# Two products pending behind the rows of the forgetting units, and the first plain gate tile issued in 16 steps behind transposes of the last six attention groups

## The chip, the cores and the metric

The kernel runs on one core of one Trainium2 chip. The metric is the device time of one execution in microseconds. Engines are named as the profile names them: PE (TensorE, the matmuls), PEld (its weight loads), DVE (VectorE), ACT (ScalarE), POOL (GpSimd) and SP (SyncE, which issues the DMAs).

## The reference

One decoder block on x of 1024 positions and 1024 channels, all in float32. Cut to what matters:

```
h = rms_norm(x, g_pre)
proj = h @ w_in
qa, ka, va, fa, za, qb, kb, vb, zb, gates = split(proj)
# forgetting attention (FoX): 8 heads of 64
log_f = log_sigmoid(fa + b_forget); c = cumsum(log_f)
P = softmax(causal(q k^T / 8 + c[t] - c[s]));  ya = (P v) * silu(za)
# differential attention: 4 heads, q1/q2 and k1/k2 of 64 with rope, v of 128
P = softmax(q1 k1^T) - lam * softmax(q2 k2^T);  yb = rms_norm(P v) * (1 - lam_init) * silu(zb)
gate_a, gate_b = split(sigmoid(gates))
merged = gate_a * (ya @ w_branch[0]) + gate_b * (yb @ w_branch[1])
out = x + rms_norm(merged @ w_out, g_post)
```

## The kernel before, in words

**Number format.** A float32 factor is cut into a high part (rounded to the matmul's float32 format, fp32r) and the rest, `hi` and `lo`. A product is three matmuls: hi with hi, hi with lo, lo with hi. So `project` (L242), which multiplies 128 columns of `w_in` with one half of the 1024 positions (a chunk of 512), is 8 x 3 = 24 matmuls of 512 columns. `load_w` (L225) loads such weights and splits them: its two flags say whether ACT or POOL makes `hi`, and whether POOL or DVE makes `lo`.

**Stages.** First x is normalized and transposed into `hT`, and V and the forget gate's logits (`fg`) are projected, to about 100 us. Then come eight attention units of two heads each: units 0 to 3 are differential, units 4 to 7 forgetting units (whose tiles have an f in their names, as the others have a d). The projections of q and k for the next unit, those of z (`z_tasks`, names `pz`, `sz`), and a few other tasks are cut into steps, which the loop at L626 puts between the attention's groups as filler; the list `ZFILL` says which z tiles belong to which unit. The last unit has two of them, z6 and z7. Attention ends at 595.5 us. Then come the gates: for the output tile d = 0 plain products (`gates_plain`, L792: two branches, two chunks, 96 matmuls), for d = 1 to 7 a Winograd scheme with eight combination tiles T that `h_load` (L804) fetches from DRAM. Then the branch products, and the output product to the end.

**A group of attention.** A group is a pair of rows of 128 queries (2g+1 and 2g in the forgetting units), with a weight of 4g+3 in the loop's count. In units 4 to 7 each group g exists for both heads (m = 0, 1), and g falls from 3 to 0. Its name is f, the unit, m, g: `f7_1_2` is unit 7, head 1, group 2. For each row `s_row` (L415) computes the scores in up to two pieces (tiles `S`, a PSUM pool of 3 banks); DVE adds the bias and reduces the minimum out of PSUM into an SBUF tile `P` (a pool of 6); ACT takes the exponential, and POOL scales it. Then `av` (L438) runs, the products of the group: `trans` (L446) transposes up to four 128x128 blocks on PE into a PSUM tile `pt` (2 banks), ACT casts it to `ph`, DVE subtracts for `pl` (3 buffers each); `prod` (L462) multiplies V with both, one step behind the transposes, into `yp` (one bank). In groups of unit 7 whose g is in `FING`, `yp` takes a bank of the scores' pool, and every second `pt` a bank of the projections' pool `pj` (2 banks). At the end `evac` adds the halves of `yp`.

**The order.** The loop at L646 runs, for each group, its rows, then the products of the group before (`pend`), then as many filler steps as are due. The tile framework's scheduler then orders the instructions of each engine by its own simulation of time, so the order in the code is not the order on an engine. `tc.issue_after(x)` keeps what is issued inside it behind the instruction x on its engine.

**The forget gate.** `forget_sums` (L590) takes log_sigmoid of `fg` in the small tile `fs` (ten operations on DVE, an Exp and an Ln on ACT), transposes it (`ft`, L615), scans it to cumulative sums and stores them for units 4 to 7. It runs at the start of unit 1 (L632).

Of the kernel before, what the change touches and what calls it, by code (L numbers as in the profile page):

```python
# [9 lines left out]
F32 = mybir.dt.float32  # L10
# [6 lines left out]
P = 128  # L17
S = 1024
D = 1024
KT = D // P  # L20
NB = S // P
CH = 512
# [4 lines left out]
UPR, DNR = slice(0, 64), slice(64, 128)  # L27
UP, DN = (0, 1, 2, 3), (3, 2, 1, 0)
GORD = (UP,) * 4 + (DN,) * 4
FING = (0,)  # L30
YORD = ((), ((4, 0), (4, 1)), ((5, 0), (5, 1), (6, 0)), ((6, 1), (7, 0), (7, 1)),
        ((0, 0), (0, 1), (1, 0)), ((1, 1), (2, 0), (2, 1)), ((3, 0), (3, 1)), ())
ZFILL = ((0,), (1,), (), (2,), (3,), (4,), (5,), (6, 7))
# [13 lines left out]
def tile_hybrid_block(  # L47
# [191 lines left out]
    def w_cols(c0):  # L239
        return w[:, c0:c0 + P].rearrange("(k p) n -> p k n", p=P)  # L240
# [10 lines left out]
    with ExitStack() as st:  # L251
# [75 lines left out]
        def z_tasks(t):  # L327
            return spill_tasks(f"z{t}", (ZA + t * P) if t < 4 else (ZB + (t - 4) * P), z_d[t])

        def spill_tasks(nm, c0, dst):  # L330
            box = {}

            def mk(c):
                def run():
                    if not box:
                        box[0] = load_w(nm, w_cols(c0))
                    ps = pj.tile([P, CH], F32, tag="pj", name=f"p{nm}_{c}")
                    project(ps, box[0], c)
                    zs = stg.tile([P, CH], F32, tag="raw", name=f"s{nm}_{c}", bufs=3)
                    nc.scalar.copy(zs, ps)  # L340
                    nc.sync.dma_start(dst[:, c * CH:(c + 1) * CH], zs)
                return run
            return [mk(0), mk(1)]
# [94 lines left out]
        def av(rows, g, vt, hoff, fox, evac, nm, final):  # L438

            if final:  # L440
                yp = sps.tile([P, CH], F32, tag="S", name=f"yp{nm}")[:, 0:2 * P]
            else:
                yp = yps.tile([P, 2 * P], F32, tag="y", name=f"yp{nm}")
            parts = {}

            def trans(jj):  # L446
                pool, tag = (pj, "pj") if final and jj % 2 else (tps, "tp")
                pt = pool.tile([P, CH], F32, tag=tag, name=f"pt{nm}_{jj}")
                ph = ptp.tile([P, CH], F32R, tag="ph", name=f"ph{nm}_{jj}")
                pl = ptp.tile([P, CH], F32R, tag="pl", name=f"pl{nm}_{jj}")  # L450
                blocks = [(2 * jj, 0), (2 * jj, 1), (2 * jj + 1, 0), (2 * jj + 1, 1)]
                if jj == g:
                    del blocks[2]
                for o, (j, r) in enumerate(blocks):
                    nc.tensor.transpose(
                        pt[:, o * P:(o + 1) * P], rows[2 * g + r][:, j * P:(j + 1) * P], ident)
                n = len(blocks) * P
                nc.scalar.copy(ph[:, 0:n], pt[:, 0:n])  # L458
                nc.vector.tensor_tensor(pl[:, 0:n], pt[:, 0:n], ph[:, 0:n], op=ALU.subtract)  # L459
                parts[jj] = ph, pl  # L460

            def prod(jj):  # L462
                ph, pl = parts[jj]
                for j in (2 * jj, 2 * jj + 1):
                    if fox:
                        v = vt[:, j, hoff:hoff + P]
                        prods = ((v, ph), (v, pl))
                    else:
                        v = vt[:, j, 0:P]
                        prods = ((v, ph), (vt[:, j, P:2 * P], ph), (v, pl))  # L470
                    odd = j % 2
                    if not odd:
                        o, src = yp, slice(0, 2 * P)
                    elif jj == g:
                        o, src = yp[:, P:2 * P], slice(2 * P, 3 * P)
                    else:
                        o, src = yp, slice(2 * P, 4 * P)
                    for n, (a, b) in enumerate(prods):
                        nc.tensor.matmul(
                            o, lhsT=a, rhs=b[:, src], start=(j == 0 and n == 0),  # L480
                            stop=(odd == 1 and jj == g and n == len(prods) - 1))

            for jj in range(g + 1 + SKEW):
                if jj <= g:
                    trans(jj)
                if jj >= SKEW:
                    prod(jj - SKEW)
            evac(yp)

        def unit_attn(u, T):  # L490

# [95 lines left out]
        nc.vector.tensor_tensor(nlam, le[:, 1:2], le[:, 0:1], op=ALU.subtract)  # L587
        nc.vector.tensor_scalar(nlam, nlam, -LAM_INIT, None, op0=ALU.add)

        def forget_sums():  # L590

            fgf = fg.rearrange("p a b -> p (a b)")
            fs = pp.tile([P, 4, 64], F32, tag="P", name="fs")
            fn, fe, fu, fc = (fs[:, n, :] for n in range(4))
            nc.vector.tensor_scalar(fn, fgf, -1.0, None, op0=ALU.mult)
            nc.vector.tensor_tensor(fn, fn, fgf, op=ALU.min)
            nc.scalar.activation(fe, fn, AF.Exp)
            nc.vector.tensor_scalar(fu, fe, 1.0, None, op0=ALU.add)
            nc.vector.tensor_scalar(fc, fu, -1.0, None, op0=ALU.add)
            nc.vector.tensor_tensor(fc, fe, fc, op=ALU.subtract)  # L600
            nc.scalar.activation(fn, fu, AF.Ln)
            nc.vector.reciprocal(fu, fu)
            nc.vector.tensor_tensor(fc, fc, fu, op=ALU.mult)
            nc.vector.tensor_tensor(fn, fn, fc, op=ALU.add)
            nc.vector.tensor_scalar(fe, fgf, 0.0, None, op0=ALU.min)
            nc.vector.tensor_tensor(fe, fe, fn, op=ALU.subtract)
            lf = pp.tile([8, S], F32, tag="P", name="lf")
            cum = pp.tile([8, S], F32, tag="P", name="cum")
            ones8 = pp.tile([8, S], F32, tag="P", name="ones8")
            nc.gpsimd.memset(ones8, 1.0)  # L610
            for half in range(2):
                tp = tps.tile([P, CH], F32, tag="tp", name=f"ft{half}")
                for q in range(4):
                        b = half * 4 + q
                        nc.tensor.transpose(tp[0:8, q * P:(q + 1) * P], fe[:, b * 8:(b + 1) * 8], ident)  # L615
                nc.scalar.copy(lf[:, half * CH:(half + 1) * CH], tp[0:8, :])
            nc.vector.tensor_tensor_scan(cum, ones8, lf, initial=0.0, op0=ALU.mult, op1=ALU.add)
            nc.vector.tensor_scalar(cum, cum, -8.0, None, op0=ALU.mult)
            nc.sync.dma_start(cum_d, cum)

        T, tasks = unit_proj(0)
        for tk in tasks:
            tk()
        pend = None
        nxt = None
        for u in range(8):  # L626
            load, load_v, groups = nxt or unit_attn(u, T)
# [13 lines left out]
            for t in SFILL[u]:  # L641
                fill += [lambda t=t, c=c: sum_squares(t, c) for c in range(2)]
                fill.append(lambda t=t: subln_scales(t))
            total = sum(s[0] for s in groups)
            done, nf = 0, 0
            for n, (wgt, rws, prd) in enumerate(groups):  # L646
# [2 lines left out]
                    vload.append(nxt[1])  # L649
                for r in rws:  # L650
                    r()
                if pend:
                    pend()
                pend = prd
                done += wgt
                while nf < len(fill) and nf < len(fill) * done / total:
                    fill[nf]()
                    nf += 1
        pend()

    bigs.close()

# [127 lines left out]
        nc.sync.dma_start(g_d[d][br][:, c * CH:(c + 1) * CH], g)  # L790

    def gates_plain(d):  # L792
        for br in range(2):
            wt = load_w(f"g{br}_{d}", w_cols(GT + br * D + d * P), True, True)
            for c in range(2):
                ps = xps.tile([P, CH], F32, tag="x", name=f"pg{d}_{br}_{c}")
# [246 lines left out]
```

## Time and profile before

| | |
|---|---|
| runs before, us | 935.11, 935.71, 936.13 (median 935.71) |
| the profiled execution, us | 938.31, of which the span is 936.2 |
| mean granted TensorE clock in the span | 0.993 |
| attention with its fillers | from about 100 to 595.5 us of the span |
| plain gate products | 595.5 to 617.5 us |
| gates of d = 1 to 7 | 617.5 to about 742 us |
| branch products, then the output product | to about 835 us, then to the end |

A group of instructions in the views below is named by engine, line, operation, and the tile written <- the tiles read, with buffer numbers left out. Times in a view are microseconds from the span's start. A busy PE can still be slower than its stream allows, because the durations of matmuls overlap.

### The profile page before, as it was taken

How to read it: one execution, taken by the hardware profiler on the slowest of the kernel's cores; microseconds unless marked ns; L12 is line 12 of the kernel's file. 1: busy time of each engine (PE TensorE's matmuls, PEld its weight loads, DVE VectorE, ACT ScalarE, POOL GpSimd, SP SyncE). 2: the span in 40 equal slices, each digit the busy share in tenths (PEclk: the TensorE clock that was granted, in tenths of full speed). 3: DMA queues.
4: the chain of work that ended last, by engine and by line, in shares of the span. 5: the costliest groups of instructions: out<-in, count | busy, mean ns of one | idle time of the engine just before them, and what ended most of it. 6: DMA issues, size and time to landing. Idle time of an engine off the chain costs nothing. (4 is left out here: it accounts for less than half of the span.)

```text
span 936.2 us, 13774 instructions
## 1 busy us (share of the span) xinstructions
PE 891.2 (95%) x4600; PEld 746.8 (80%) x4600; DVE 627.0 (67%) x1180; ACT 437.1 (47%) x862; POOL 493.6 (53%) x461
## 2 busy tenths in 40 slices
PE   7999999989999999999999999999999999999993
PEld 5899986777887878888878887788888878887872
DVE  6731257878888778577667568426778892559766
ACT  3421125555756684565755657524444451224331
POOL 7200034645645458373644566417676336978963
PEclk9999999999999999999999999999999999999997
DMA  8532336324335253534444342596655595201332
GB/s 315 185 136 92 113 106 177 104 75 130 103 86 150 72 180 104 156 123 128 146 153 129 97 161 72 224 395 192 210 164 159 187 363 192 84 30 46 112 113 90
DMA packets 118664, 136.95 MB, mean 146 GB/s; under 512 B 10545, under 2 KB 84273, under 8 KB 117570
## 3 DMA queue, kind: packets, MB, share of 16 engines
q1 hardware_dynamic: 118594, 136.08, 45.9%
q8 instruction: 36, 0.59, 0.3%
q14 instruction: 34, 0.28, 0.1%
HBM read 85.65 MB, written 37.81 MB: 132 GB/s over the span
## 5 line engine op out<-in xcount | busy, mean ns | idle before, releaser
L195 PE MATMUL pv<-wvhi,hT 128*128 128x264 f32 (+2 forms) x384 | 88.9, 323 | 0.4 <-DVE hT L181 0.4
L246 PE MATMUL pz<-hT,hi_z 128*128 128x512 f32 x256 | 83.9, 394 | 0.0
L246 PE MATMUL pk<-hT,hi_k 128*128 128x512 f32 x256 | 81.1, 394 | 2.0 <-DVE KB L298 2.0
L246 PE MATMUL pq<-hT,hi_q 128*128 128x512 f32 x256 | 82.3, 394 | 0.0
L727 PE MATMUL x_o<-wo_op,a_o 128*128 128x512 f32 x336 | 78.3, 392 | 3.4 <-POOL a_o L679 2.2
L861 PE MATMUL pb<-yT,hi_br 128*128 128x512 f32 x256 | 78.6, 389 | 0.0
L727 PEld LDWEIGHTS x_o<-wo_op,a_o 128*128 128x128 f32 x336 | 62.7, 188 | 18.8 <-POOL a_o L679 3.4
L727 PE MATMUL x_g<-T,a_g 128*128 128x512 f32 x336 | 77.5, 390 | 0.0
L727 PEld LDWEIGHTS x_g<-T,a_g 128*128 128x128 f32 x336 | 63.1, 188 | 13.3
L195 PEld LDWEIGHTS pv<-wvhi,hT 128*128 128x128 f32 x384 | 64.3, 189 | 6.1 <-DVE hT L181 0.7
L433 ACT ACTIVATE Pd<-Pd,mxd 128x128 f32<-128x128 f32 (+7 forms) x64 | 49.5, 775 | 34.4 <-DVE mxd L428 33.7
L549 POOL TENSOR_SCALAR Pf<-Pf,lf 128x1024 f32<-128x1024 f32 (+3 forms) x64 | 50.4, 790 | 28.3 <-DVE lf L435 23.9
L519 POOL TENSOR_SCALAR Pd<-Pd,ld 128x128 f32<-128x128 f32 (+7 forms) x32 | 26.1, 817 | 73.8 <-DVE ld L518 41.4
L545 POOL TENSOR_TENSOR cb<-cb,trim 128x128 f32<-128x128 f32 x64 | 31.9, 499 | 60.2 <-DVE mxf L428 39.7
L433 ACT ACTIVATE Pf<-Pf,mxf 128x1024 f32<-128x1024 f32 (+3 forms) x64 | 49.8, 777 | 27.4 <-DVE mxf L428 24.9
L195 PE MATMUL pv<-wvlo,hT 128*128 128x512 f32 (+2 forms) x192 | 61.8, 324 | 0.6 <-DVE wvlo L151 0.6
L727 PE MATMUL x_g<-hT,a_g 128*128 128x512 f32 x252 | 58.6, 390 | 0.0
L459 DVE TENSOR_TENSOR plf<-ptf,phf 128x512 fp32r<-128x512 f32 (+1 forms) x80 | 49.8, 634 | 10.9 <-ACT phf L458 10.2
L246 PEld LDWEIGHTS pk<-hT,hi_k 128*128 128x128 f32 x256 | 47.3, 188 | 12.0 <-DVE KB L298 2.4
L861 PEld LDWEIGHTS pb<-yT,hi_br 128*128 128x128 f32 x256 | 48.0, 188 | 10.1 <-DVE cu_g L720 0.2
L727 PEld LDWEIGHTS x_g<-hT,a_g 128*128 128x128 f32 x252 | 47.3, 188 | 10.0
L246 PEld LDWEIGHTS pq<-hT,hi_q 128*128 128x128 f32 x256 | 47.4, 188 | 9.0
(248 smaller groups left out, 2427.7 us busy)
## 6 DMA issues: line engine op xcount, KB each, us to landing
t_d<-t SPq DMA_DIRECT2D x32, 256.0 KB, 2.1
T<-t_d SPq DMA_DIRECT2D x8, 1024.0 KB
raw<-in_w_in_dram SPq DMA_DIRECT2D x14, 512.0 KB, 4.4
vb_d<-vbs SPq DMA_DIRECT2D x8, 512.0 KB
va_d<-vas SPq DMA_DIRECT2D x8, 512.0 KB, 4.0
raw_k<-in_w_in_dram SPq DMA_DIRECT2D x8, 512.0 KB, 4.7
raw_q<-in_w_in_dram SPq DMA_DIRECT2D x8, 512.0 KB
V<-vb_d SPq DMA_DIRECT2D x4, 1024.0 KB
```

The lines of the kernel that those rows point to most:

```text
L195: nc.tensor.matmul(ps[n], lhsT=hT[hp][k // 4][i // 4][:, k % 4, hs], rhs=wt[k][:, a:b], start=first, stop=(k == KT - 1 and hp == 1))
L246: nc.tensor.matmul(ps, lhsT=a[:, k, :], rhs=hT[h][k // 4][c][:, k % 4, :], start=(k == 0 and a is hi and h == 0), stop=(k == KT - 1 and a ...
L433: nc.scalar.activation(pr[:, 0:n], pr[:, 0:n], AF.Exp, bias=mx[:, len(pcs) - 1:len(pcs)], scale=-1.0, accum_out=le)
L459: nc.vector.tensor_tensor(pl[:, 0:n], pt[:, 0:n], ph[:, 0:n], op=ALU.subtract)
L519: nc.gpsimd.tensor_scalar(p2[:, 0:n], p2[:, 0:n], l2, 1.0, op0=ALU.mult, op1=ALU.mult)
L545: nc.gpsimd.tensor_tensor(diag, diag, trim, op=ALU.add)
L549: nc.gpsimd.tensor_scalar(p1[:, 0:n], p1[:, 0:n], l1, 1.0, op0=ALU.mult, op1=ALU.mult)
L727: nc.tensor.matmul(x[m], lhsT=a[:, ai, k, :], rhs=right[m][bi][k], start=(k == 0 and n == 0), stop=(k == 3 and n == 2))
L861: nc.tensor.matmul(ps, lhsT=a[:, kk, :], rhs=yT[g][h][:, k % 2, sl], start=(k == 0 and a is hi and h == 0), stop=(k == 3 and a is lo))
```

## The change

The products of a group stand two groups behind its rows in units 4 to 7 (one behind in units 0 to 3, as before). The first of the two plain gate tiles, `g0_0`, is taken out of `gates_plain`, and its 48 matmuls become 16 steps of three. Each step is issued behind the last transpose of a piece of one of the last six groups of unit 7, as the table `PINNED` says. Its weights are now split by POOL (`hi`) and DVE (`lo`), where before ACT made `hi` and POOL `lo`. Its PSUM tiles come from the pool `pj`, and ACT takes the sigmoid inside the attention's last part. `FING` gains the group 1. The logarithms of the forget gate become a function of their own, `forget_logs`, which is the fourth filler step of unit 0, and its tile `fs` moves to another pool.

```
-FING = (0,)
+FING = (0, 1)
+PINNED = {"f7_0_2": (1, 1, 1), "f7_1_2": (1, 1, 1), "f7_0_1": (2, 1), "f7_1_1": (2, 1), "f7_0_0": (2,),
+          "f7_1_0": (2,)}
...
+        def gate_spill(c, ps, zs):
+            nc.scalar.activation(zs, ps, AF.Sigmoid)
+            nc.sync.dma_start(g_d[0][0][:, c * CH:(c + 1) * CH], zs)
...
                 for o, (j, r) in enumerate(blocks):
-                    nc.tensor.transpose(
+                    last = nc.tensor.transpose(
                         pt[:, o * P:(o + 1) * P], rows[2 * g + r][:, j * P:(j + 1) * P], ident)
+                if nm in PINNED:
+                    with tc.issue_after(last.ins):
+                        for _ in range(PINNED[nm][jj]):
+                            pins.pop(0)()
...
+        def gate_steps():
+            box = {}
+            def step(c, k):
+                if not box:
+                    box["w"] = load_w("g0_0", w_cols(GT))
+                if k == 0:
+                    box[c] = pj.tile([P, CH], F32, tag="pj", name=f"pg0_0_{c}")
+                hi, lo = box["w"]
+                for a, h in ((hi, 0), (hi, 1), (lo, 0)):
+                    nc.tensor.matmul(
+                        box[c], lhsT=a[:, k, :], rhs=hT[h][k // 4][c][:, k % 4, :],
+                        start=(k == 0 and a is hi and h == 0), stop=(k == KT - 1 and a is lo))
+                if k == KT - 1:
+                    zs = stg.tile([P, CH], F32, tag="raw", name=f"sg0_0_{c}", bufs=3)
+                    gate_spill(c, box[c], zs)
+            return [lambda c=c, k=k: step(c, k) for c in range(2) for k in range(KT)]
+        pins = gate_steps()
...
-        def forget_sums():
+        fgs = {}
+        def forget_logs():
             fgf = fg.rearrange("p a b -> p (a b)")
-            fs = pp.tile([P, 4, 64], F32, tag="P", name="fs")
+            fs = fgs[0] = stg.tile([P, 4, 64], F32, tag="raw", name="fs", bufs=3)
...
             nc.vector.tensor_tensor(fe, fe, fn, op=ALU.subtract)
+        def forget_sums():
+            fe = fgs[0][:, 1, :]
             lf = pp.tile([8, S], F32, tag="P", name="lf")
...
-        pend = None
+        pend = []
...
+            if u == 0:
+                fill.insert(3, forget_logs)
...
-                if pend:
-                    pend()
-                pend = prd
+                pend.append(prd)
+                while len(pend) > (1 if u < 4 else 2):
+                    pend.pop(0)()
...
-        pend()
+        for prd in pend:
+            prd()
+        while pins:
+            pins.pop(0)()
...
     def gates_plain(d):
-        for br in range(2):
+        for br in range(1, 2):
```

A parameter `out` that `spill_tasks` gains is used by no caller.

How the change moves instructions shows at three places. In the rows below, S are scores, pt transposes, yp products, the number at the end of a name is the buffer's, and "x2" means two in a row. The first place is PE's order among the first rows of unit 7; `pz7_1` is the second half (positions 512 to 1023) of the last z tile. Before:

```order
L246 MATMUL pz7_1_6680<-hT101_93,hi_z7_6580 128x512
L426 MATMUL Sf7_0_7_1_6186<-KA7_5390,TA7_5388 128x512
L427 MATMUL Sf7_0_7_1_6186<-KA7_5390,X0f7_3_6177 128x512
L246 MATMUL pz7_1_6680<-hT001_89,lo_z7_6581 128x512
L246 MATMUL pz7_1_6680<-hT001_89,hi_z7_6580 128x512
L246 MATMUL pz7_1_6680<-hT101_93,hi_z7_6580 128x512
L246 MATMUL pz7_1_6680<-hT001_89,lo_z7_6581 128x512
L479 MATMUL ypf6_0_1_6041<-phf6_0_1_0_6043,V6_5146 128x256
```

And the same place after the change:

```order
L248 MATMUL pz7_0_6541<-hT110_94,hi_z7_6537 128x512
L248 MATMUL pz7_0_6541<-hT010_90,lo_z7_6538 128x512
L435 MATMUL Sf7_0_7_1_6169<-KA7_5373,TA7_5371 128x512
L436 MATMUL Sf7_0_7_1_6169<-KA7_5373,X0f7_3_6160 128x512
L492 MATMUL ypf6_0_1_6070<-phf6_0_1_0_6072,V6_5103 128x256
L492 MATMUL ypf6_0_1_6070<-plf6_0_1_0_6073,V6_5103 128x256
```

The 24 matmuls of `pz7_1`, which stood around the scores of row 7, now stand behind the first transposes of the group f7_0_2, and the first half `pz7_0` stands here.

The second place is PE's order around the transposes of the group f7_1_2, in the last part of attention; `pg0_0_0` is the first chunk of the gate tile. Before:

```order
L455 MATMUL ptf7_1_2_1_6647<-ident_69,Pf7_1_5_6506 128x128
L426 MATMUL Sf7_1_1_0_6824<-KB7_5391,TB7_5389 128x256
L427 MATMUL Sf7_1_1_0_6824<-KB7_5391,X1f7_0_6819 128x256
L455 MATMUL ptf7_1_2_2_6660<-ident_69,Pf7_1_4_6521 128x128
L455 MATMUL ptf7_1_2_2_6660<-ident_69,Pf7_1_5_6506 128x128 x2
L479 MATMUL ypf7_1_2_6637<-phf7_1_2_0_6639,V7_5934 128x256
L479 MATMUL ypf7_1_2_6637<-plf7_1_2_0_6640,V7_5934 128x256
```

And after the change:

```order
L464 MATMUL ptf7_1_2_1_6719<-ident_69,Pf7_1_5_6450 128x128
L514 MATMUL pg0_0_0_6608<-hT010_90,hi_g0_0_6604 128x512
L514 MATMUL pg0_0_0_6608<-hT110_94,hi_g0_0_6604 128x512
L514 MATMUL pg0_0_0_6608<-hT010_90,lo_g0_0_6605 128x512
L435 MATMUL Sf7_0_0_0_6775<-KA7_5373,TA7_5371 128x128
L436 MATMUL Sf7_0_0_0_6775<-KA7_5373,X0f7_0_6759 128x128
L464 MATMUL ptf7_0_1_1_6802<-ident_69,Pf7_0_2_6584 128x128
L464 MATMUL ptf7_0_1_1_6802<-ident_69,Pf7_0_3_6573 128x128 x2
L492 MATMUL ypf7_1_2_6706<-phf7_1_2_0_6708,V7_5891 128x256
L492 MATMUL ypf7_1_2_6706<-plf7_1_2_0_6709,V7_5891 128x256
```

Three gate matmuls stand behind the transposes, and between a group's transposes and its products there now stand scores and transposes of later groups.

The third place is SP's queue of DMAs ahead of the loads of the T tiles; `g_d0_0` is where the first gate tile is stored, `y_d6` and `y_d7` where attention's results are, `sz7_1` is a z tile's second half. Before:

```order
L562 DMA y_d6_105<-ys6_0_6168 128x256
L562 DMA y_d7_106<-ys7_3_6373 128x256
L562 DMA y_d7_106<-ys7_2_6574 128x256
L562 DMA y_d7_106<-ys7_1_6759 128x256
L810 DMA T40_6903<-t_d4_0_133 128x2048
L810 DMA T41_6904<-t_d4_1_134 128x2048
```

And after the change:

```order
L350 DMA z_d7_132<-sz7_1_6678 128x512
L861 DMA raw1_1_7055<-in_w_in_dram 128x8x128
L334 DMA g_d0_0_107<-sg0_0_0_6797 128x512
L596 DMA y_d7_106<-ys7_2_6649 128x256
L334 DMA g_d0_0_107<-sg0_0_1_6926 128x512
L854 DMA T40_6965<-t_d4_0_133 128x2048
L854 DMA T41_6966<-t_d4_1_134 128x2048
```

The two stores of the gate tile, which stood behind the T loads, now stand ahead of the first of them, the second directly.

More of the change, by code (lines that the diff above doesn't have):

```diff
@@ L328, in z_tasks, with spill_tasks @@
             return spill_tasks(f"z{t}", (ZA + t * P) if t < 4 else (ZB + (t - 4) * P), z_d[t])
-        def spill_tasks(nm, c0, dst):
+        def gate_spill(c, ps, zs):
+            nc.scalar.activation(zs, ps, AF.Sigmoid)
+            nc.sync.dma_start(g_d[0][0][:, c * CH:(c + 1) * CH], zs)
+        def spill_tasks(nm, c0, dst, out=None):
             box = {}
@@ L339, in run @@
                     zs = stg.tile([P, CH], F32, tag="raw", name=f"s{nm}_{c}", bufs=3)
+                    if out:
+                        out(c, ps, zs)
+                        return
                     nc.scalar.copy(zs, ps)
```

## The prediction

> **What bounds the kernel now.** I read the page first, then the busy time by stretch, then who waits for whom on TensorE (PE), and last the order of the instructions around those places.
>
> ```profile
> span 936.2 us, 13774 instructions
> PE 891.2 (95%) x4600; PEld 746.8 (80%) x4600; DVE 627.0 (67%) x1180; ACT 437.1 (47%) x862; POOL 493.6 (53%) x461
> ```
>
> PE is busy for 95% of the span, so a change pays only where PE stands still. The stretches show where that is (columns: stretch, its length, then busy us and count of PE, PEld, DVE, ACT, POOL, the granted PE clock, the DMA share, GB/s).
>
> ```profile
> 546.00:557.00 11.00, 11.00 (x60) 9.44 (x59) 8.32 (x17) 5.80 (x14) 8.07 (x7) 1.00 0.67 215
> 557.00:579.00 22.00, 19.79 (x119) 16.21 (x117) 19.59 (x58) 16.85 (x33) 14.15 (x18) 0.92 0.31 97
> 579.00:595.50 16.50, 13.82 (x100) 11.41 (x98) 12.88 (x41) 13.16 (x35) 8.22 (x15) 1.00 0.06 21
> 595.50:617.50 22.00, 22.00 (x99) 18.23 (x98) 2.54 (x4) 5.29 (x9) 5.93 (x5) 1.00 1.00 396
> ...
> 160.00:170.00 10.00, 9.12 (x47) 7.35 (x48) 9.02 (x22) 6.27 (x14) 6.38 (x7) 1.00 0.61 149
> 170.00:180.00 10.00, 8.49 (x43) 6.59 (x42) 9.58 (x17) 4.82 (x10) 5.00 (x3) 1.00 0.42 115
> ...
> 190.00:200.00 10.00, 7.49 (x43) 5.89 (x42) 9.37 (x21) 4.93 (x8) 4.85 (x4) 1.00 0.36 87
> ```
>
> From 557 to 595.5, the end of attention, PE idles 2.2 + 2.7 = 4.9 us, and VectorE (DVE) is busy for 19.59 of 22.00 us in the first of the two stretches. From 595.5 on, in the gates, PE has no idle time at all. Around 160 to 200 us it idles again, with DVE at 90% or more in the rows shown.
>
> ```profile
> PE Sf L426 <- DVE mxf L428: 1.7, 2, 0.9
> PE ptf L455 <- DVE plf L459: 1.5, 3, 0.7
> PE ypf L479 <- DVE ys L559: 0.5, 2, 0.3
> PE ypf L479 <- DVE plf L459: 0.4, 2, 0.2
> PE ypf L479 <- ACT phf L458: 0.3, 1, 0.3
> ```
>
> These are PE's waits from 557 to 596 (total us, times, longest): scores wait until DVE has read a score bank, transposes until DVE has emptied theirs, products for the split rows. It is a chain of latencies, which other matmuls could fill.
>
> Busy time understates the loss, since matmuls overlap. Start to start they take less than the duration shown:
>
> ```profile
> 595.40:617.40 22.00, 21.92 (x96) 17.95 (x96) 1.79 (x3) 1.00 1.00 396
> 586.22 0.29 PE L479 MATMUL ypf<-plf,V 128*128 128x256 f32 x1
> 586.34 0.28 PE L479 MATMUL ypf<-phf,V 128*128 128x256 f32 x1
> ...
> 587.17 0.60 PE L455 MATMUL ptf<-ident,Pf 128*128 128x128 f32 x4
> 587.53 0.37 PE L479 MATMUL ypf<-phf,V 128*128 128x256 f32 x1
> ```
>
> The 96 plain gate matmuls take 22.0 us, 0.229 us each; a 256-wide product takes about 0.117, a transpose 0.107 on the average over the attention (four of them stand in the 0.36 us from 587.17 to 587.53, where the next matmul starts early). A 384-wide matmul is 0.172 and a 128-wide one 0.06, in the proportion of the columns.
>
> **The change, part by part.** *The gate tile.* 48 matmuls leave the gates and stand among the attention's last transposes; 48 x 0.229 = 11.0 us is all that can be gained by that, if the attention does not end later. But the second half of the last z tile (24 matmuls, 5.5 us) moves too: before, it lies ahead of most of unit 7, and now behind the first transposes of the group f7_0_2. So I split unit 7 at those transposes, which end at 578.6 before.
>
> Behind the split, the order has 48 gate and 24 z matmuls, and of attention 42 of 256 columns, 2 of 384, 18 of 128 and 38 transposes: 72 x 0.229 + 42 x 0.117 + 2 x 0.172 + 18 x 0.06 + 38 x 0.107 = 16.5 + 4.9 + 0.3 + 1.1 + 4.1 = 26.9 us. Waits in this part were 2.7 us without filler; I take half, 1.3, the bounds being 0 and 2.7. ScalarE (ACT) gets two more loads of its function table here, around the first gate chunk's sigmoid, and the second chunk's stands at the end:
>
> ```profile
> L789 ACT ACT_TABLE_LOAD x1 | 1.3, 1283 | 0.0
> L789 ACT ACTIVATE g<-pg 128x512 f32<-128x512 f32 x4 | 2.4, 595 | 4.4 <-PE pg L246 4.4
> ```
>
> Table, sigmoid and table are 1.28 + 0.60 + 1.28 = 3.2 us. Queued behind them are the split of the transposed block f7_1_1_0 and the exponentials of rows 1 and 0, for which f7_1_0's transposes wait; between the transposes of f7_0_1_0 and those stand 27 gate matmuls' worth of PE work and more (over 6 us), so I cost the loads at nothing. Without that cover they would cost up to 3.2.
>
> Ahead of the split, PE has 34 matmuls of 512 columns, 10 of 384, 50 of 256, 10 of 128 and 43 transposes: 7.8 + 1.7 + 5.9 + 0.6 + 4.6 = 20.6 us from the first score matmul of row 7 (546.5) on. DVE sets the pace here, so the question is how much earlier it gets through.
>
> ```profile
> 545.16 2.84 POOL L236 TENSOR_TENSOR lo_g<-raw_g,hi_g 128x1024 fp32r<-128x1024 f32 x1
> ...
> 551.95 1.76 POOL L364 TENSOR_TENSOR f<-hT,hT 128x512 f32<-128x512 f32 x1
> ...
> 553.75 0.86 DVE L384 TENSOR_TENSOR f<-f,f 128x512 f32<-128x512 f32 x1 [1.09 <-POOL f L364]
> ...
> 556.65 0.69 DVE L371 TENSOR_TENSOR t<-f,t 128x512 fp32r<-128x512 f32 x1 [1.43 <-DMA t_d<-t]
> 557.26 0.74 DVE L428 CUSTOM_DVE_ANT_0 Pf<-Sf,cb,mxf 128x512 f32<-128x512 f32 x1
> ...
> 578.48 0.56 DVE L459 TENSOR_TENSOR plf<-ptf,phf 128x384 fp32r<-128x384 f32 x1
> ```
>
> Row 7's second reduction starts at 557.26. Ahead of it lie a sum that waited 1.09 for GpSimd (POOL), and a subtraction that waited 1.43 for a DMA. POOL's subtraction of 2.84 us for the gate tile leaves POOL for DVE, and in the new order the reduction stands ahead of the late subtraction (1.43 + 0.69 saved). New ahead of it is the evacuation of f6_0_1, whose products PE reaches at 546.5 + 0.5 + 14 x 0.229 + 0.5 = 550.7; with 0.9 of products, a copy, that evacuation (0.45), the sum (0.86) and a split (0.56), the reduction starts near 553.5: some 4 us sooner. The bounds are 0 and 5.4 (all three waits and the late subtraction gone). From there to 579.0 DVE took 21.8 us with 2.4 idle in the stretch. ACT's z copy and split of the second gate weights, and POOL's second 2.84, leave this stretch, so I take 1.0 less; the bounds are 0 and 2.4. The split then comes at 578.6 - 4.0 - 1.0 = 573.6, and the next gate chunk starts at 573.6 + 26.9 + 1.3 = 601.8. Before, it started at 595.5 + 11.0 = 606.5. **Gain 4.7 us.** The bounds: 578.6 - 5.4 - 2.4 + 26.9 = 597.7, a gain of 8.8; and 578.6 + 26.9 + 2.7 = 608.2, a loss of 1.7.
>
> *The logarithms of the forget gate.* Their chain leaves the start of unit 1 for unit 0.
>
> ```profile
> 199.50 0.60 PE L615 MATMUL ft<-ident,fs 128*8 128x128 f32 x4 [1.77 <-DVE fs L606]
> ```
>
> This wait of 1.77 us should go. But the chain, with its two table loads of 1.28 us on ACT, then lies at about 160 to 170 us, where DVE is busy 9.02 and 9.58 of 10. I take a gain of 0.8, with bounds of -1.8 (the wait goes, nothing comes back) and +1.8 (it comes back there).
>
> *Products two groups behind* in units 4 to 7. They move no work; PE hardly waits in units 4 to 6. I take 0.5 of gain, bounds -1 and +2 (below). *FING* gives four groups a score bank instead of one, with no work of its own; its use lies in the tail above.
>
> Sum: -4.7 - 0.8 - 0.5 = **-6.0 us**. The profiled execution took 938.31 us, its span 936.2 plus 2.1 around it, 2.6 above the median of 935.71; the difference holds for either, so the forecast is 932.3 for such an execution and **929.7** for the median.
>
> **The clock.**
>
> ```profile
> 560.40:563.90 3.50, 1.77 (x7) 0.89 (x6) 2.85 (x10) 3.27 (x7) 3.50 (x2) 0.99 0.78 270
> 563.90:567.30 3.40, 3.40 (x17) 3.17 (x15) 3.28 (x11) 1.78 (x4) 3.40 (x6) 0.50 0.55 137
> ```
>
> After 3.5 us in which PE was busy half of the time, its longest wait being 0.9, it ran at half clock for 3.4 us, which takes 1.7 us of its work away. Unit 7's front has no z filler now, so this can happen again there. PE has 27 - 20.6 = 6.5 us to spare in it, so I cost one such window at nothing. The Trainium skill, in "TensorE: Matmul & The Clock Gate", Part 1, says that the clock falls after at least one idle window of about 3.4 us; by that rule it would not have fallen here, nor would it after, and the sum would be the same with no risk at this place. The trace does not agree with it (0.50 after a wait of 0.9), so the risk stays in the range.
>
> **The rivals.** *The idle time only moves to the front.* DVE is 89% busy from 557 to 579, so unit 7 may take as long from its first row as before. Then the split stays near 578.6, and only the early parts are left: 606.8 against 606.5, less 1.3, so 934.7. Against it: three things ahead of the reduction are gone or later.
>
> *The transfers of the gates become late.*
>
> ```profile
> 594.83 1.46 SPq L810 DMA_DIRECT2D T<-t_d  x3
> 601.80:617.00 15.20, 15.20 (x69) 12.59 (x68) 0.69 (x1) 2.23 (x5) 1.29 (x1) 1.00 1.01 419
> ```
>
> The eight T tiles, 8.4 MB, go out from 594.83, 0.7 ahead of the attention's end, at 419 GB/s: 20 us. The gate product that reads the last pair came 22.0 + 60 x 0.229 = 35.7 us behind that end, and comes 11.0 sooner now, at 24.7. On SP's queue the first T now stands behind the store of the second gate chunk, which waits for two casts (1.2), the table (1.28) and the sigmoid (0.60): T starts some 2.2 us behind the attention's end, and the last lands near 22.2 to 24. It just fits; if the start slips by 2 us, PE waits 1.5 there: 931.2.
>
> *Slower: the row tiles are full.* There are six P tiles, two for a group. With two groups pending, the next group's rows take the last two, and a reduction waits for transposes three groups back.
>
> ```profile
> DVE Pf L428 <- PE ptf L455: 14.0, 10, 4.4
> ```
>
> Such waits stood at 14.0 us in ten places already, where two tiles were still spare. Units 4 to 7 have 32 groups. From 6.0 / 32 = 0.19 us of PE time lost for each group the gain is gone; at 0.3 us the kernel loses 9.6 and gains 6.0: 939.3. Against it: the new order puts the releasing transposes ahead of the waiting rows, and PE's waits in units 4 to 6 were few.
>
> **How the numbers follow.** The forecast, with the sum's gain of 2 us or more, has 0.68; the moved idle time 0.14; late transfers 0.08; full row tiles 0.10. A difference under 0.2% (1.9 us) can't be told from no change. Forecast and late transfers are faster, and a little of the moved idle time: 0.77. The rest of that makes 0.13 for the same, and 0.10 is slower. For the range, the gains' ends are 8.8 + 1.8 + 1 = 11.6 together, hardly all at once, so I stop at 10.7: 925.0. Above, the moved idle time with its bounds (934.7 + 1.8) goes to 936.5, and the full row tiles are left out.
>
> **What would show it.** Right: hardly any PE idle time in the last 27 us of attention; row 7's second reduction about 4 us sooner after row 7's first score; the split nearer to 27 than to 32 us behind that; no wait at the `ft` transposes; no wait for a T tile. Wrong: PE idle time of over 8 us between row 7's first score and the split, more waits of reductions for transposes in units 4 to 6, half clock over several windows, or PE waiting in the gates for a DMA.

## The result, and the profile after

The changed kernel takes **946.60 us** (median of 4 runs, 945.01 to 951.07) against 935.92 for the kernel before on the same chip: a ratio of **1.0125 [1.0096, 1.0155]**, slower by about 1.2%. A second submission of the same kernel gave 946.22 against 935.75, 1.0103 [1.0070, 1.0136]. The profiled execution took 945.01, its span 943.2; for before it was 938.31 and 936.2, so these two traces hold 7.0 us of the difference.

The page of after, the two lines on the span and the engines:

```profile
span 943.2 us, 13769 instructions
...
PE 895.1 (95%) x4600; PEld 747.6 (79%) x4600; DVE 625.5 (66%) x1181; ACT 437.7 (46%) x863; POOL 492.5 (52%) x461
```

As many matmuls as before. PE is busy 3.9 us longer and ACT 0.6, the other engines less. So the time is not in added work. The stretches around unit 7, cut at row 7's first score (547.66 in after, 546.47 in before), at the split of the prediction (577.95 and 578.58, where the last of its transposes starts), and at the first matmul of the second plain gate tile (605.99 and 606.45). First after, then before, with the columns of the prediction's stretches:

```profile
547.60:557.10 9.50, 7.94 (x44) 6.22 (x42) 8.19 (x20) 5.48 (x13) 7.47 (x7) 1.00 0.60 187
557.10:578.00 20.90, 18.26 (x107) 14.48 (x107) 18.41 (x57) 15.36 (x31) 11.46 (x17) 0.92 0.26 89
578.00:606.00 28.00, 28.00 (x175) 24.76 (x173) 13.92 (x40) 18.73 (x40) 11.78 (x18) 1.00 0.16 48
```

```profile
546.50:557.20 10.70, 10.70 (x56) 9.10 (x55) 8.11 (x17) 5.32 (x13) 7.57 (x7) 1.00 0.66 217
557.20:578.50 21.30, 19.09 (x114) 15.55 (x114) 18.89 (x58) 16.40 (x32) 13.69 (x17) 0.92 0.32 99
578.50:606.40 27.90, 25.22 (x152) 20.95 (x150) 15.23 (x43) 16.49 (x39) 13.32 (x19) 1.00 0.43 160
```

The third stretch is what the change was made of: PE is now busy for all of its 28.0 us. But the two stretches ahead of it, 30.4 us instead of 32.0, did not shrink as the prediction had it. PE idles 4.2 us in them (2.2 before), and DVE is busy for 26.6 of the 30.4 us (27.0 of 32.0 before). All in all the second gate tile starts at 605.99 instead of 606.45: nearly nothing.

From there to the end, PE's waits in after (line, what was waited for, total us, times, longest), then in before:

```profile
PE pb L905 <- ACT hi_br L234: 3.1, 1, 3.1
PE x_o L771 <- POOL a_o L723: 2.0, 2, 1.1
PE x_o L771 <- ACT a_o L722: 1.2, 2, 0.9
PE x_g L771 <- DVE a_g L723: 0.9, 1, 0.9
PE pb L905 <- POOL lo_br L238: 0.4, 1, 0.4
PE pb L905 <- DVE cu_g L764: 0.2, 1, 0.2
```

```profile
PE x_o L727 <- POOL a_o L679: 2.2, 2, 1.2
PE x_o L727 <- ACT a_o L678: 1.3, 2, 1.0
PE pb L861 <- POOL lo_br L236: 0.9, 1, 0.9
```

No wait names a T tile. New are the 3.1 at the first branch product, some 150 us behind the change, and 0.9 in the last gate pair. The order there, ACT and PE in after:

```profile
747.63 0.64 ACT L829 ACTIVATE zs<-zs 128x512 f32<-128x512 f32 x1 [4.24 <-POOL yd L828]
749.93 0.63 ACT L829 ACTIVATE zs<-zs 128x512 f32<-128x512 f32 x1 [1.67 <-POOL yd L828]
750.47 3.87 ACT L894 CAST yT<-yf 128x1024 fp32r<-128x1024 f32 x4
754.25 1.04 ACT L234 CAST hi_br<-raw_br 128x1024 fp32r<-128x1024 f32 x1
...
743.89 8.35 PE L771 MATMUL x_g<-hT,a_g 128*128 128x512 f32 x36
755.34 1.31 PE L905 MATMUL pb<-yT,hi_br 128*128 128x512 f32 x4 [3.11 <-ACT hi_br L234]
```

and in before:

```profile
742.66 0.63 ACT L785 ACTIVATE zs<-zs 128x512 f32<-128x512 f32 x1 [4.12 <-POOL yd L784]
744.96 0.63 ACT L785 ACTIVATE zs<-zs 128x512 f32<-128x512 f32 x1 [1.67 <-POOL yd L784]
745.50 3.89 ACT L850 CAST yT<-yf 128x1024 fp32r<-128x1024 f32 x4
749.28 1.06 ACT L232 CAST hi_br<-raw_br 128x1024 fp32r<-128x1024 f32 x1
...
742.85 8.35 PE L727 MATMUL x_g<-hT,a_g 128*128 128x512 f32 x36
751.03 1.55 PE L861 MATMUL pb<-yT,hi_br 128*128 128x512 f32 x6
```

ACT's order here is the last two sigmoids of `y_work` (the finish of the attention outputs), four casts to `yT`, then the cast of the branch weights `hi_br`, which PE needs. In before that cast ends at 750.34 and PE arrives at 751.03: nearly level, with 0.7 us of room. In after the same queue runs 5.0 us later, PE only 1.0, and PE stands still. Then the clock falls:

```profile
750.00:755.00 5.00, 2.24 (x10) 1.50 (x8) 4.61 (x6) 5.00 (x6) 0.00 (x0) 1.00 0.99 327
755.00:765.00 10.00, 9.07 (x25) 6.36 (x26) 10.00 (x8) 6.14 (x8) 5.42 (x2) 0.66 1.01 357
756.30:763.10 6.80, 6.21 (x15) 4.19 (x14) 6.80 (x5) 4.84 (x6) 4.48 (x2) 0.50 1.00 358
```

The mean of 0.66 over 10 us is half clock for 6.8 us, which by estimate costs some 3.4 us more. The output product starts at 846.4 instead of 839.3 (about 835 in the table of before is too early): 7.1 us, the whole difference of these two traces.

### The profile page after: what moved, and what is told of

The parts are those of the page before. It is cut to its first block, busy times and chain, and to the rows that moved or that the text cites. A ratio compares the mean times of both kernels' runs of the same rounds, so it can differ in the third digit from the quotient of the medians.

```text
span 943.2 us, 13769 instructions
## 1 busy us (share of the span) xinstructions
PE 895.1 (95%) x4600; PEld 747.6 (79%) x4600; DVE 625.5 (66%) x1181; ACT 437.7 (46%) x863; POOL 492.5 (52%) x461
## 5 line engine op out<-in xcount | busy, mean ns | idle before, releaser
L905 PE MATMUL pb<-yT,hi_br 128*128 128x512 f32 x256 | 80.9, 398 | 3.3 <-ACT hi_br L234 3.1
L583 POOL TENSOR_SCALAR Pf<-Pf,lf 128x1024 f32<-128x1024 f32 (+3 forms) x64 | 52.9, 829 | 33.0 <-DVE lf L444 30.0
L579 POOL TENSOR_TENSOR cb<-cb,trim 128x128 f32<-128x128 f32 x64 | 29.5, 463 | 65.2 <-DVE mxf L437 50.7
L553 POOL TENSOR_SCALAR Pd<-Pd,ld 128x128 f32<-128x128 f32 (+7 forms) x32 | 26.9, 841 | 67.7 <-DVE ld L552 32.7
```

The source lines that it names most:

```text
L553: nc.gpsimd.tensor_scalar(p2[:, 0:n], p2[:, 0:n], l2, 1.0, op0=ALU.mult, op1=ALU.mult)
L579: nc.gpsimd.tensor_tensor(diag, diag, trim, op=ALU.add)
L583: nc.gpsimd.tensor_scalar(p1[:, 0:n], p1[:, 0:n], l1, 1.0, op0=ALU.mult, op1=ALU.mult)
L905: nc.tensor.matmul(ps, lhsT=a[:, kk, :], rhs=yT[g][h][:, k % 2, sl], start=(k == 0 and a is hi and h == 0), stop=(k == 3 and a is lo))
```

## The experiments

"Ratio" is time over that of the kernel before in the same batch, with its 95% interval.

**The change's parts, one undone at a time.** First the logarithms, back at unit 1's start with their old tile:

```diff
-            fs = fgs[0] = stg.tile([P, 4, 64], F32, tag="raw", name="fs", bufs=3)
+            fs = fgs[0] = pp.tile([P, 4, 64], F32, tag="P", name="fs")
...
             if u == 1:
+                forget_logs()
                 forget_sums()
...
-            if u == 0:
-                fill.insert(3, forget_logs)
```

> The changed kernel with one part undone: the forget gate's logarithms run again at the start of unit 1, right ahead of the sums. Theory L (the logarithms in unit 0 cost more DVE and ACT time there than their wait was worth; in the trace PE lost 2.0 us more than before by the end of unit 3, though the 1.8 us wait was gone): about 944.6 us, 2.0 less than the 946.6 of the changed kernel, with the wait of the transposes for fs back and the lost 2.0 gone by the end of unit 3. Rival (the loss in units 1 to 3 is chance or comes from elsewhere): within 1 us of 946.6.

942.23, 1.0059 [1.0039, 1.0079]: 4 us less than the second submission of after (1.0103), 6 less than the first, where the expectation had 2. These ran in other batches; a comparison within one batch comes below.

Then the gate tile, back in the gates (`FING = (0,)`, `pins = []`, `for br in range(2)`); logarithms and depth 2 as in after.

> The changed kernel with the gate tile back behind attention (no pinned steps, FING as before); the logarithms in unit 0 and the two pending products stay. Theory T (the loads of the T tiles start where attention ends, and what follows them, the weights of the second pair and its operands on POOL, ACT and DVE, reaches the branch as late as PE does; with 11 us of gate work moved ahead of these loads that chain ends some 6 us late): the branch wait is gone, 935.9 + 2.1 (logarithms) - 0.6 (two pending) = 937.4. Rival R (the wait at the branch comes from something else that the change did): 946.6 + 1.9 (what unit 7 gained) = 948.5.

943.58, 1.0064 [1.0043, 1.0085]: between the expectations. PE's wait at the branch is gone and the gates run in before's order, so the wait belongs to the moved gate tile. The time doesn't come back all the same, because 63.9 us pass from row 7's first score to the second gate tile, against 60.0 in before: in this one trace, products two groups behind, without the gate matmuls to fill, make unit 7 longer by 4.

**What makes the branch late?** In after the T loads go out at 607.61 instead of 594.83, and POOL starts the sums of the second gate pair at 636.88 instead of 630.57 (after, then before):

```profile
607.61 0.88 SPq L854 DMA_DIRECT2D T<-t_d  x2
636.88 1.32 POOL L735 TENSOR_TENSOR S_g<-raw 128x512 f32<-128x512 f32 x1
...
630.57 1.32 POOL L691 TENSOR_TENSOR S_g<-raw 128x512 f32<-128x512 f32 x1 [2.85 <-DMA raw<-in_w_in_dram]
```

One kernel issues that pair's weights ahead of the last T tiles:

```diff
-    h_load()
+    t_load = h_load()
...
+            with tc.issue_after(raw_load(2)):
+                t_load((5, 7))
```

> The changed kernel with nothing undone, but the two weight loads of the second gate pair issued ahead of the last four of the eight T tiles (the sums of the first pair's weights are formed a step earlier for this). Theory T: these weights land some 10 us sooner, POOL starts on the second pair that much sooner, PE does not wait at the first branch product, and the time is about 946.6 - 7.1 = 939.5. Rival R: the wait of 3.1 at the first branch product stays, 946.6. If the last T tiles come late now: a wait of PE for a T tile near 630.

944.93, 1.0088 [1.0060, 1.0117]. POOL started 11 us sooner, at 625.55, and `hi_br` still came at 754.70. PE waited for it 0.8 us instead of 3.1, since it came later itself: it had waited in the gates for T tiles:

```profile
PE x_g L772 <- DMA T<-t_d: 3.4, 2, 1.9
```

Next, **before** with a single load, half of the second pair's weights, put behind four loads of y:

```diff
+            if d == 2 and br == 1:
+                with tc.issue_after(y_dma[7]):
+                    nc.sync.dma_start(r, w_cols(GT + br * D + d * P))
```

> The kernel before, with one DMA moved: the second half of the second gate pair's weights is issued behind the four loads of y for units 4 to 7, some 5 us later than before. No computation changes. Theory T: the operand chain of the gates has no slack at the branch, so the first branch product comes 4 to 6 us later and the time is 940 to 942, though attention and PE's gate products are untouched. Rival R: the gates absorb it, within 1 us of 935.9.

946.11, 1.0103 [1.0072, 1.0135]: one DMA issued 4.5 us later (626.28 instead of 621.79) costs 9 to 10 us, twice the expectation and as much as the whole change. Its trace at the branch is that of after:

```profile
754.66 1.04 ACT L232 CAST hi_br<-raw_br 128x1024 fp32r<-128x1024 f32 x1
...
755.75 2.71 PE L864 MATMUL pb<-yT,hi_br 128*128 128x512 f32 x6 [3.30 <-ACT hi_br L232]
```

The changed kernel itself ran once more (the second submission, 1.0103), beside the next three kernels:

> The changed kernel once more, unaltered, as the anchor on this chip for the three beside it: 946.6, with units 1 to 3 up to 2 us other than in the first profile (two profiles of this same part of the program differed by that much), and hi_br on ACT near 754.

Is it the number of bytes in the queue? Two of four T pairs are not loaded, and the other two are read in their place, so that 4.2 MB less move:

```diff
-        for m in (4, 6, 5, 7):
+        for m in (4, 6):
...
+        h_ops[5], h_ops[7] = h_ops[4], h_ops[6]
```

> The changed kernel without the loads of four of the eight T tiles (T5 and T7 are left out, their products read T4 and T6 instead, so 4.2 MB less move behind attention and the gates of d = 1 to 7 are not the reference's). Theory T, sharpened (what is late is the backlog of T, weights and y that can start only when attention ends, some 50 us at 400 GB/s; it pushes the weights and operands of every later pair): the backlog ends 10 us sooner, hi_br stands at 749 to 750 again, no wait at the first branch product, 939.5. Rival R (some order of ACT's casts holds hi_br at 754, whatever moves): 946.6 with hi_br at 754.

944.85, 1.0086 [1.0054, 1.0118]. The theory of late bytes falls:

```profile
626.25 1.31 POOL L735 TENSOR_TENSOR S_g<-raw 128x512 f32<-128x512 f32 x1 [15.30 <-DMA raw<-in_w_in_dram]
...
753.40 1.04 ACT L234 CAST hi_br<-raw_br 128x1024 fp32r<-128x1024 f32 x1
754.50 2.70 PE L906 MATMUL pb<-yT,hi_br 128*128 128x512 f32 x6 [2.92 <-ACT hi_br L234]
```

Eleven us of lead at the second pair are less than one at the branch. In the trace the lead is lost between the fourth and the fifth pair, where POOL's order has y multiplications between a pair's sums and the operands made of them. The fifth pair's weights are loaded only behind that (673.22, against 676.33 in after), and POOL waits 6.41 us for them. Two kernels moved the y loads (those of units 0 to 3, and two of x) later, behind the weights of the fourth and of the seventh pair, alone and with the second pair's weights first:

```diff
+        if d == 4:
+            with tc.issue_after(last.ins):
+                for t in (0, 1, 2, 3):
+                    y_load(t)
```

> The changed kernel with the loads of y for units 0 to 3 (2.1 MB) and of two x tiles for the end (0.5 MB) put behind the weights of the fourth and seventh pair; T and the second pair's weights stay as they are. Theory T: the third pair's weights land some 5 us sooner, the second pair's do not, so only part of the lag goes: 943, hi_br at 751 to 754. Rival R: 946.6.

> Both: the second pair's weights ahead of the last four T tiles, and the loads of y of units 0 to 3 and of the two x tiles put later. Theory T: POOL starts on the second pair near 626 and on the third by 648, hi_br at 749 to 750, no wait for T above 1 us, 939.5. Rival R: hi_br at 754 and 946.6.

946.40, 1.0109 [1.0079, 1.0138], and 944.17, 1.0106 [1.0059, 1.0153]: neither helps measurably. In the trace of the second, PE waits 1.6 us for `hi_br`, which comes at 753.02, and 1.9 for a T tile.

So `hi_br` comes late however early the second pair starts. What is left is ACT's order at the branch itself. The work on the last y tile moves behind the casts of `yT2`, `yT3` and the first branch weights, which don't need it:

```diff
-        ((0, 0), (0, 1), (1, 0)), ((1, 1), (2, 0), (2, 1)), ((3, 0), (3, 1)), ())
+        ((0, 0), (0, 1), (1, 0)), ((1, 1), (2, 0), (2, 1)), (), ())
...
+    yt_casts(2, eslot[0:2])
+    yt_casts(3, eslot[2:4])
+    wbr0 = br_w(0, 0)
+    y_work(3, 0)
+    y_work(3, 1)
+    yt_casts(0, hslot[0, 0])
+    yt_casts(1, hslot[1, 0])
```

> The changed kernel with the work on the last y tile (t = 3, two pieces) put behind the first branch weights and the casts of yT 2 and 3, which no longer stand behind its two sigmoids on ACT; T, weights and all else stay as they are. Theory Y (PE waits at the branch because hi_br stands on ACT behind these sigmoids, whose chain, rb from DRAM, DVE, POOL, runs 5 us later than before; the transfers only make that chain late): hi_br by 748, no wait above 1 us at the branch, clock back at 1.00 there, 946.3 - 7 = 939.3. Rival T (the weights and operands themselves are late at the branch): the wait stays at 2 to 3 us, 945 to 946.

940.92, **1.0039 [1.0022, 1.0057]**: some 6 us of the loss are gone (1.0103 - 1.0039 of 936). `hi_br` comes 4.9 sooner, PE does not wait for it, and the clock is 1.00 from 750 to 765:

```profile
745.59 3.90 ACT L895 CAST yT<-yf 128x1024 fp32r<-128x1024 f32 x4
749.39 1.04 ACT L234 CAST hi_br<-raw_br 128x1024 fp32r<-128x1024 f32 x1
...
754.36 1.52 PE L920 MATMUL pb<-yT,hi_br 128*128 128x512 f32 x6
```

The same edit in before, where no wait for `hi_br` stands there to be removed:

> The same edit in the kernel before. Theory Y: only the 0.9 us wait for lo_br at the branch can go, 935 to 936. If the edit itself brings time in both kernels alike, it says nothing of the change: then some 929.

936.40, 0.9990 [0.9976, 1.0004]: nothing. And on the kernel with the late weight load:

> e5 (the kernel before with the second half of the second pair's weights loaded behind y, which made it 9 to 10 us slower) with the reorder of e10 added: the last y tile's work stands behind the first branch weights. Theory Y: the late weights still push every later pair's operands by 5 us, but PE no longer waits at the branch, so nearly all of the 9 to 10 us goes: 937 to 938. Rival (late weights cost PE time in the gates themselves): 942 or more.

939.66, 1.0024 [1.0000, 1.0048]: some 7 of its 9 to 10 us go. One late DMA and the moved gate tile lose their time at the same place.

**The rest.** With the last y tile moved, the logarithms back as well:

> e10 with the logarithms back at the start of unit 1. Theory L (the logarithms in unit 0 cost 1.5 to 3 us by the end of unit 3; seven profiles with them there lost 34.5 us of PE time in the mean by then, three without 32.7): 2 us less than e10, 937.3. Rival: as e10.

937.80, **1.0004 [0.9986, 1.0022]**: the logarithms in unit 0 cost 3.1 us, and what is left of the change, gate tile, depth 2 and `FING`, can't be told from nothing. Then depth 1 in all units, on top of that:

```diff
-                while len(pend) > (1 if u < 4 else 2):
+                while len(pend) > 1:
```

> e12 with one product pending again in units 4 to 7, so only the pinned gate tile and FING are left of the change. Theory D (two pending products leave units 4 to 6 as they were, 10.9 us lost against 11.1, but cost unit 7 its front): unit 7 loses 2 to 3 us less, 935. Rival (two pending products are what lets the pinned steps fill the tail): 1 us or more above e12.

943.82, 1.0063 [1.0041, 1.0085]: 6.0 us slower where a gain was expected. Behind the split 37.6 us pass instead of 28.0. The gate matmuls follow transposes which now come close behind their rows, and PE waits there (540 to 625 us):

```profile
PE ptf L464 <- POOL Pf L583: 2.6, 3, 1.3
PE pg L248 <- ACT sg L333: 2.0, 1, 2.0
PE ypf L492 <- DVE plf L472: 1.6, 4, 0.9
```

So depth 2 and the gate steps need each other: depth 2 alone costs some 3 to 4 us (1.0064 less the 0.0035 of the logarithms; 3.9 in unit 7 of that trace), the gate steps alone 6, both together nothing measurable. `FING` was not undone by itself.

Why does unit 7's front not get shorter by more? One suspect was the gate weights' split, now POOL's and DVE's, where DVE waits 1.59 us and then takes 2.32 close ahead of row 7. It goes back to ACT and POOL:

```diff
-                    box["w"] = load_w("g0_0", w_cols(GT))
+                    box["w"] = load_w("g0_0", w_cols(GT), True, True)
```

> e12 with the gate tile's weights split by ACT and POOL again, as before the change (hi by ACT, lo by POOL). Theory F (the front of unit 7 gained 1.3 us instead of 4 because DVE now has the 2.3 us subtraction of these weights ahead of row 7's second reduction): that reduction comes 2 us sooner after row 7's first score, 7.5 us instead of 9.5, and the time is 2 us under e12, 935.8. Rival: the reduction stays where it is, since the sums of h on POOL or PE's order hold it, and the time is e12's 937.8.

938.95, 1.0019 [1.0000, 1.0038], no better: row 7's second reduction starts 10.94 us behind the first score (9.50 in after, 9.51 in the kernel that this edit is made on). The suspect is cleared. The other idea takes the front's length as given and gives PE its z matmuls back there, by making unit 7's filler due twice as early:

```diff
-                while nf < len(fill) and nf < len(fill) * done / total:
+                while nf < len(fill) and nf < len(fill) * done * (2 if u == 7 else 1) / total:
```

> e12 with the last z tile's steps due earlier in unit 7, so that its second half stands among the first rows of unit 7 again, as before the change. Theory Z (without it PE has nothing to do in the front while DVE works: 1.8 us idle from 552 to 558, half clock from 558 to 563): the front loses 2 us less, the tail behind f7_0_2_0 waits 0.5 to 1 more, together 936.5. Rival: DVE paces the front whatever PE has to do, so 24 matmuls there only take filler from the tail: e12's 937.8 or 1 more.

935.87 against 938.27, **0.9972 [0.9960, 0.9984]**: the only version that is faster than before. Before with the last y tile moved had 0.9990 [0.9976, 1.0004], and against that a gain is not shown, since the intervals overlap. The stretches, cut as above but at its own times:

```profile
546.00:558.00 12.00, 12.00 (x64) 10.23 (x63) 10.03 (x23) 6.13 (x13) 7.45 (x8) 1.00 0.58 188
558.00:579.60 21.60, 17.54 (x109) 14.78 (x108) 18.24 (x51) 15.31 (x32) 13.03 (x17) 0.92 0.32 98
579.60:603.50 23.90, 22.84 (x152) 20.43 (x150) 14.48 (x40) 18.73 (x40) 10.81 (x17) 1.00 0.07 24
```

Row 7's first 12 us are filled again. The split comes 34.06 us behind row 7's first score, and the part behind it takes 23.87 instead of 28.04: 57.92 in sum, 58.34 in after and 59.72 in the kernel that this edit is made on. Both edits together:

> Both edits on e12. Theories F and Z together: 934.5, the first version faster than the kernel before by more than 0.2%. If neither holds: 938 or more.

936.87, 0.9994 [0.9979, 1.0009]: the weights' split on ACT and POOL gives most of the gain back.

## Why the prediction was wrong, by its own steps

*The part behind the split came out, in part by luck.* 26.9 us of matmuls and 1.3 of waits were forecast, 28.2 together; after took 28.04. That PE would have no idle time there was right, and the two table loads cost nothing visible. But no wait is left, and the same 172 matmuls took 28.0 from start to start, most of the difference in the 512-wide ones (17.5 instead of 16.5): errors of 1.1 and 1.3 us stand against each other.

*The part ahead of it failed first.* The step was "the reduction starts near 553.5: some 4 us sooner", and with it "The split then comes at 578.6 - 4.0 - 1.0 = 573.6". Counted from row 7's first score, the second reduction moved from 10.79 to 9.50, 1.3 sooner, and the split from 32.11 to 30.29, where the forecast was 27.1. The late subtraction did go behind the reduction, as forecast, and the waits ahead of the reduction fell from 1.09 + 1.43 to 0.54 + 0.64. But DVE's work ahead of it did not become less, 8.2 us (8.1 before): besides the new evacuation and split, the first sum (0.85, at 549.05), which ran ahead of row 7 in before (544.89), runs behind its first score in after. And the evacuation of f6_0_1 came late:

```profile
551.88 0.28 PE L492 MATMUL ypf<-phf,V 128*128 128x256 f32 x1
...
553.92 0.37 ACT L592 COPY yt<-ypf 64x256 f32<-64x256 f32 x1
...
554.87 0.73 DVE L380 TENSOR_TENSOR t<-f,t 128x512 fp32r<-128x512 f32 x1 [0.64 <-ACT phf L471]
555.64 0.42 DVE L593 TENSOR_TENSOR ys<-ypf,yt 64x256 f32<-64x256 f32 x1
...
557.16 0.74 DVE L437 CUSTOM_DVE_ANT_0 Pf<-Sf,cb,mxf 128x512 f32<-128x512 f32 x1
```

PE began its products 4.2 us behind the first score, exactly as forecast. The forecast had the evacuation right behind them and a copy, some 5.5 behind the first score at the latest; it started 8.0 behind, after a copy that stood on ACT behind an exponential and a cast, and a subtraction with its wait on DVE. I summed PE's work (20.6 us) and followed one chain, but not what ACT and DVE do in between.

One trace says little here. Over the nine profiles with the new order of unit 7, its z tile behind the split and the gate weights split as in after, the split comes 30.3 to 32.3 behind row 7's first score, 31.15 on the mean, and the second gate tile 59.2; over the four with before's order it is 31.6 and 59.5. So of the forecast gain of 4.7 us some 0.3 are there: of 1.1 won at the reduction, 0.7 are lost again by the split and 0.2 behind it. This is the rival "the idle time only moves to the front", to which I gave 0.14. Taking the 24 z matmuls out of this part, 5.5 us of PE work, shortened it by 2.9 at most: with them back in front the split comes at 34.06.

*The clock* fell to 0.50 for 3.4 us in before (from 563.9) and in after (from 558.3); both kernels show a mean of 0.92 in that stretch, so it cost the change nothing there, as assumed. It fell again where I had not looked, at the branch.

*The logarithms* were the term "a gain of 0.8, with bounds of -1.8 ... and +1.8". Measured: 3.1 us lost (1.0039 to 1.0004). The wait at `ft` did go, as forecast. But the wait went only from that place:

```profile
PE Sd L435 <- DVE mxd L437: 2.8, 3, 1.4
PE ptd L464 <- POOL Pd L556: 0.9, 1, 0.9
PE ypd L492 <- DVE pld L472: 0.3, 1, 0.3
```

These are PE's waits from 190 to 250 us in after, 4.0 us; in before they were 3.9 with `ft`'s 1.8 among them. And 160 to 170 us has PE busy for 8.22 of 10 instead of 9.12, with DVE at 9.71:

```profile
160.00:170.00 10.00, 8.22 (x42) 6.22 (x40) 9.71 (x26) 8.74 (x16) 6.17 (x6) 1.00 0.43 98
```

So the cost seems to have moved to two other places, at both of which DVE is busy nearly all the time or waited for; that it is the same chain is read from the traces, not tested. Row 7's first score starts at 547.7 on the mean of eight profiles with the logarithms in unit 0, and at 544.9 on that of ten with them at unit 1: 2.8 us, all ahead of unit 7.

*Late transfers, and the step that put the sign wrong.* The sum had no term for the branch at all, and the rival priced late transfers only as a wait for a T tile in the gates (1.5 us, 931.2). T did start behind the attention's end (607.61), and no product waited for a T tile; "It just fits" held. I followed the transfers only to the first matmul that reads them. What they delay goes on: the second pair's weights, the operands that POOL, DVE and ACT make, the y pieces, and at the end the cast of `hi_br`. In before, this chain was 0.7 us ahead of PE at 751, hidden under a PE without a wait all through the gates; a slip of 5.0 us there became 3.1 of wait and, by estimate, some 3.4 by half clock. That this place costs 6 to 7 us, and that ACT's order there decides it, is shown by the moved y tile (6 us back in after, 7 with the late load, nothing in before). That the late transfers start it is shown for before, with one weight load (1.0103); in after, where the wait comes with the moved gate tile, an earlier start of the second pair alone did not undo it. That POOL's order eats that lead is read from one trace, not tested, so which of the late transfers delays the branch in after stays open.

*Row tiles full* did not come: PE's waits from 320 to 540 us sum to 2.9 us in after and 4.1 in before, and depth 2 with the gate steps costs nothing measurable.

The account, from the measured ratios of 936: 1.0103 for the change is 0.0064 at the branch (6.0 us), 0.0035 by the logarithms (3.3), and 0.0004 for gate tile and depth 2. The intervals of these ratios are some 0.002 to 0.003 to either side, so each term is good to 2 to 4 us; by the first submission (1.0125) the branch would have 8.0. The forecast had -6.0 from the gate tile, depth and logarithms, and nothing at the branch.

## What to carry to other kernels

A stage in which PE is 100% busy can hide a chain that ends just level with it. Before moving work out of such a stage, or loads behind its start, find on each engine what ends last at the stage's end, and how long before PE comes. Here 0.7 us were left, and a slip of 5.0 cost 3.1 of waiting and some 3.4 more at half clock. When such a chain is too late, look in the engine's order for an item that stands ahead of a needed one without being needed yet: here, moving it won 6 us, and earlier transfers won hardly anything. Filler that was taken out of a stretch in which DVE was busy for 27 of 32 us made that stretch shorter by 2.9 us at most, and by 0.5 against before, not by the 5.5 of its own work; the idle time stayed, and the filler took its time elsewhere.

## What was not expected of the hardware

One weight load of the second gate pair, issued 4.5 us later, behind four loads of y, cost 9 to 10 us in before, and PE stood still 130 us further on. After one wait of 3.1 us at the branch, with PE busy for 2.24 of the 5 us around it, the clock was 0.50 for 6.8 us, so the wait cost about twice its length; in the second submission it was 0.50 for 3.4 us after a wait of 3.2. The Trainium skill, in "TensorE: Matmul & The Clock Gate", Part 1, speaks of an idle window of about 3.4 us; the 3.1 at the branch is near to that, while the 0.50 in the prediction's rows, after a longest wait of 0.9, does not agree with it if the window must be idle throughout. Over the 18 traces the clock fell 35 times between 90 and 900 us, always to 0.50 and for 3.4 or 6.8 us, and PE's longest idle time in the 6.8 us ahead was 0.6 to 3.3 us.
